# Feed-forward activations turned by VectorE's 32 x 32 blocks and a round trip through DRAM instead of on TensorE

## The chip, the cores and the metric

The kernel runs on one core of a Trainium2 chip. The metric is the device time of one execution in microseconds (us). Within a core TensorE (PE) multiplies, VectorE (DVE) and ScalarE (ACT) work elementwise, GpSimd (POOL) does a few side jobs, and SyncE (SP) issues nearly all DMA transfers, one after the other in program order. PEld is TensorE's weight load, which overlaps its matmuls.

## What is computed

A decoder trunk of two layers on 256 tokens of width 1024 (fp32). Each layer is a feed-forward block, a token mixing block and a second feed-forward block, so there are four feed-forward blocks in all:

```
def swiglu(h, w_gate, w_up, w_down):
    return (jax.nn.silu(h @ w_gate) * (h @ w_up)) @ w_down
for l in range(DEPTH):                                   # DEPTH = 2, FFN_HIDDEN = 2816
    h = rms_norm(x, ffn1_norm[l])
    x = x + 0.5 * swiglu(h, ffn1_w_gate[l], ffn1_w_up[l], ffn1_w_down[l])
    ...                                                  # mixing: S5, sparse and forgetting attention
    h = rms_norm(x, ffn2_norm[l])
    x = x + 0.5 * swiglu(h, ffn2_w_gate[l], ffn2_w_up[l], ffn2_w_down[l])
return rms_norm(x, final_norm)
```

## The kernel before

Every large product is made at more than half precision from two parts: a weight tile `raw` arrives by DMA, ACT copies it to `hi` (rounded), and DVE forms `lo = raw - hi`. The activations are split likewise. TensorE then runs three matmuls (hi x hi, lo x hi, hi x lo) for every 128 rows of the inner dimension and every 128 tokens.

**Units.** `plan` (line 78) cuts all weights into units of at most 2 x 128 rows by 512 columns, in the order of use. `feed_dma` (line 347), `feed_hi` and `feed_lo` issue a unit's load on SP, its `hi` on ACT and its `lo` on DVE. There are 4 `raw` buffers, 5 `hi` and 4 `lo`: a load waits until the `lo` of the unit four earlier is done, a `hi` until TensorE has finished the unit five earlier, a `lo` until it has finished the unit four earlier. A full unit is 512 KB and 12 matmuls of 512 columns.

**Feed-forward block** (`ffn`, line 616). The hidden width 2816 is cut into five chunks of 512 columns and one of 256. For each chunk TensorE makes gate and up products for both halves of the tokens (8 units, 96 matmuls). ACT writes `s` = silu(gate), and DVE writes `act` = up x s (`scalar_tensor_tensor`, two instructions, one for each half of the tokens). The down product needs `act` with the hidden index on the partitions. The generator `up_T` (line 627) brings this about: for every two blocks of 128 hidden columns, four TensorE transposes against the identity `ident` write a PSUM bank `ps_t`, ACT copies the bank to `ath` and DVE writes `atl = ps_t - ath`. `ath` and `atl` are the stationary side of the down product, which runs over d = 0, 1 (two halves of the output columns) and within each over 22 blocks of 128 hidden rows, 11 units.

**Order.** All engines' instructions are written out by hand in program order. Between matmuls `tick` (line 325) asks a model clock (`Clock`) which waiting generator can go on, and steps it. A generator that yields a tile goes on once the model says that the tile is ready. Each engine then runs its own instructions strictly in that order and waits on semaphores for the real data. An ACT or DVE instruction whose data is late holds up the `hi` or `lo` behind it, and a DMA whose data is late holds up the loads behind it on SP. In layer 0's first block, generators that prepare the mixing (`prep_once`, `prep_bias`, `prep_layer`) fill DVE's free time as well.

Of the kernel before, what the change touches and what calls it, by code (L numbers as in the profile page):

```python
# [9 lines left out]
F32 = mybir.dt.float32  # L10
F32R = mybir.dt.float32r
I32 = mybir.dt.int32
AF = mybir.ActivationFunctionType
OP = mybir.AluOpType
# [4 lines left out]
P = 128  # L19
T = 256  # L20
# [3 lines left out]
FK = F // P  # L24
L = 2
H = 6
HD = 64
# [46 lines left out]
def f_chunks():  # L74
    return [(c, min(512, F - c)) for c in range(0, F, 512)]


def plan(a):

    units = []  # L80

    def add(w, k0, nk, c0, n):
        k = k0
        while k < k0 + nk:
            m = min(2 if len(units) > 1 else 1, k0 + nk - k)
            units.append((w[k * P:(k + m) * P, c0:c0 + n].rearrange("(k p) c -> p k c", p=P), m, n))
            k += m

    def ffn(l, which):
        wg, wu, wd = (a[f"{which}_w_{n}"][l] for n in ("gate", "up", "down"))  # L90
        for i, (c0, n) in enumerate(f_chunks()):
            order = [(wg, 0), (wu, 0), (wg, 4), (wu, 4)] if i == 0 else [(wg, 0), (wg, 4), (wu, 0), (wu, 4)]
            for w, k0 in order:
                add(w, k0, 4, c0, n)
        for d in range(2):
            for k0 in range(0, FK, 4):
                add(wd, k0, min(4, FK - k0), d * 512, 512)

    def mix(l):
        w = a["w_in"][l]  # L100
        for k0 in (0, 4):
            add(w, k0, 4, X0, XW)
            add(w, k0, 4, U0, 256)
        for c0, n in ((V0, VW), (QC0, 512), (QC0 + 512, 256), (QB0, 384)):
            for k0 in (0, 4):
                add(w, k0, 4, c0, n)
        for kind, name, d in ORDER:
            if kind == "gate":
                for k0 in (0, 4):
                    add(w, k0, 4, G0 + GATE[name] * D + d * 512, 512)  # L110
            elif kind == "glu":
                add(a["ssm_w_glu"][l], 0, 2, 0, 512)
            else:
                add(a[f"w_branch_{name}"][l], 0, BRANCH_K[name], d * 512, 512)
        for k0 in (0, 4):
            for d in range(2):
                add(a["w_out"][l], k0, 4, d * 512, 512)

    for l in range(L):
        ffn(l, "ffn1")  # L120
        mix(l)
        ffn(l, "ffn2")
    return units
# [110 lines left out]
class Trunk:  # L234
# [381 lines left out]
    def ffn(self, nxt):  # L616
        nc, tc = self.nc, self.tc
        self.hT = self.nexthT
        ss = self.ss
        self.new_ss()  # L620
        with tc.tile_pool(name="ffn", bufs=1, side="left") as pool:
            ath = pool.tile([P, FK, T], F32R, name="ath")
            atl = pool.tile([P, FK, T], F32R, name="atl")
            rstd = None
            pend = None

            def up_T(act, k0, nk):
                yield act
                for b in range(0, nk, 2):
                    i, ps = yield from self.bank()  # L630
                    for j in range(2):
                        for t in range(2):
                            nc.tensor.transpose(ps[:, j * T + t * P:j * T + t * P + P],
                                                act[:, t, (b + j) * P:(b + j + 1) * P], self.ident)
                    yield ps
                    h, lw = ath[:, k0 + b:k0 + b + 2], atl[:, k0 + b:k0 + b + 2]
                    p3 = ps.rearrange("p (k t) -> p k t", k=2)
                    nc.scalar.activation(h, p3, AF.Copy)
                    nc.vector.tensor_tensor(lw, p3, h.bitcast(F32), op=OP.subtract)
                    self.tfree(i)  # L640

            for ci, (c0, n) in enumerate(f_chunks()):
                if ci == 0:
                    self.finish(*self.h_gens[:1])
                    pg = self.acc()
                    self.mm_tok(pg, self.hx, 0, 4, n, 0, 7)
                    pu = self.acc()
                    self.mm_tok(pu, self.hx, 0, 4, n, 0, 7)
                    self.finish(*self.h_gens)
                    self.mm_tok(pg, self.hx, 4, 2, n, 0, 7)  # L650
                    while not self.summed:
                        self.step(self.s_gens[0])
                    rstd = self.rstd_of(ss)
                    self.mm_tok(pg, self.hx, 6, 2, n, 0, 7)
                else:
                    pg = self.acc()
                    self.mm_tok(pg, self.hx, 0, 4, n, 0, 7)
                    self.mm_tok(pg, self.hx, 4, 4, n, 0, 7)
                s = pool.tile([P, 2, 512], F32, tag="s", name="s")
                act = pool.tile([P, 2, 512], F32, tag="act", name="act", bufs=2)  # L660
                for t in range(2):
                    nc.scalar.activation(s[:, t, :n], pg[t][:, :n], AF.Silu, scale=rstd[:, t:t + 1])
                if ci == 0:
                    self.mm_tok(pu, self.hx, 4, 4, n, 0, 7)
                else:
                    pu = self.acc()
                    self.mm_tok(pu, self.hx, 0, 4, n, 0, 7)
                    self.mm_tok(pu, self.hx, 4, 4, n, 0, 7)
                for t in range(2):
                    nc.vector.scalar_tensor_tensor(act[:, t, :n], pu[t][:, :n], rstd[:, t:t + 1], s[:, t, :n],  # L670
                                                   op0=OP.mult, op1=OP.mult)
                if pend:
                    self.finish(pend)
                pend = self.spawn(up_T(act, c0 // P, n // P), -1)
            ax = lambda k: (ath[:, k], atl[:, k])
            gens = []
            for d in range(2):
                ps = self.acc()
                last = nxt is None and d == 1
                for k0 in range(0, FK - LAST if last else FK, 2):  # L680
                    if d == 0 and k0 + 2 > FK - 2:
                        self.finish(pend)
                    self.mm_tok(ps, ax, k0, 2, 512, 0, FK - 1)
                if last:
                    self.last_chunk(ps, ax)
                    return
                gens.append(self.chunk_done(ps, d, 0.5, nxt))
            self.h_gens = [g for g in gens if g]
# [818 lines left out]
```

## Time and profile before

| | |
|---|---|
| median of 3 runs | 1172.56 us (1171.79 to 1173.34) |
| the profiled execution | 1173.79 us, its span 1172.0 us |
| PE busy | 1157.6 us (99%) |
| PEld busy | 973.8 us (83%) |
| DVE busy | 784.0 us (67%) |
| ACT busy | 608.2 us (52%) |
| POOL busy | 85.7 us (7%) |
| DMA | 208.07 MB, mean 178 GB/s; the main queue's packets take 55.5% of the 16 engines' span |

Busy PE is not PE at its peak, since matmuls are pipelined: a matmul of 512 columns is shown as 0.39 us long, but the next one starts 0.227 us later. What a stretch of matmuls costs is therefore read from start to start. The rows used below come from the page, from the waits (who waited for whom), the chain of work that ended last in order of time, the instructions in order of time, the groups of instructions, and the busy times by stretch. L217 is the helper line through which all engine calls go.

### The profile page before, as it was taken

To read this page: it belongs to the slowest core of one execution; us is meant where nothing else is said; L and a number is where in the kernel's file an instruction comes from. 1 tells how busy PE (TensorE), PEld (TensorE's weight loads), DVE (VectorE), ACT (ScalarE), POOL (GpSimd) and SP (SyncE) were. 2 spreads that over 40 slices of the span, in tenths; PEclk is the share of its full clock that TensorE was granted. 3 is DMA by queue.
4 is the path that set the end of the run, shared out by engine and by line. 5 is a ranking of instruction groups with operands and counts; after the bars stand their busy time and mean duration, and the time that the engine had idled before them with its cause. 6 is when DMAs were issued, how large, how long until landed. Compare 5 with 4: busy or idle time off the path is not lost.

```text
span 1172.0 us, 16482 instructions
## 1 busy us (share of the span) xinstructions
PE 1157.6 (99%) x5990; PEld 973.8 (83%) x5990; DVE 784.0 (67%) x1380; ACT 608.2 (52%) x905; POOL 85.7 (7%) x135
## 2 busy tenths in 40 slices
PE   8999999999999999999999999999999999999997
PEld 6888888998787888888888888889987788888885
DVE  4876975798777665555578646558977776555554
ACT  5544454644765554444455545446548655444442
POOL 1000700000210700000000000000013000000000
PEclk9999999999999999999999999999999999999999
DMA  7656655466444666646566546544744456655661
GB/s 270 223 173 178 209 162 178 153 189 183 124 149 152 193 198 190 184 146 223 193 189 181 174 143 221 185 150 146 234 128 140 157 189 197 190 179 162 206 193 69
DMA packets 115554, 208.07 MB, mean 178 GB/s; under 512 B 7486, under 2 KB 27376, under 8 KB 115472
## 3 DMA queue, kind: packets, MB, share of 16 engines
q1 hardware_dynamic: 114000, 203.51, 55.5%
q0 software_dynamic: 1184, 3.11, 1.0%
q8 instruction: 47, 0.77, 0.3%
q10 hardware_dynamic: 288, 0.39, 0.1%
q14 instruction: 35, 0.29, 0.1%
HBM read 205.91 MB, written 1.07 MB: 177 GB/s over the span
## 4 chain that ended last, share of the span: by engine, by line
PE 96%; ACT 2%; DVE 1%; DMA 1%; issue 0%; SPq 0%; ACTq 0%; DVEq 0%
PE ps_acc L217 88%; PE ps_t L217 8%; DMA raw<-in_ffn_w_gate_dram 1%; ACT vT L217 1%; ACT hi L217 0%; ACT st L217 0%; DVE lo L217 0%; SPq L217 0%; DVE st L217 0%; ACT ahl L217 0%; DVE rsqt L217 0%; DVE bl L217 0%; DVE rstd L217 0%; ACT bh L217 0%; ACT junk L217 0%
## 5 line engine op out<-in xcount | busy, mean ns | idle before, releaser
L217 DVE TENSOR_TENSOR lo<-raw,hi 128x1024 fp32r<-128x1024 f32 (+3 forms) x415 | 468.5, 1136 | 228.7 <-PE ps_acc L217 190.2
L217 ACT ACTIVATE hi<-raw 128x1024 fp32r<-128x1024 f32 (+3 forms) x415 | 408.3, 989 | 356.2 <-PE ps_acc L217 278.2
L217 PE MATMUL ps_acc<-hi,h0h 128*128 128x512 f32 (+3 forms) x544 | 212.1, 390 | 2.7 <-ACT hi L217 2.6
L217 PE MATMUL ps_acc<-hi,h1h 128*128 128x512 f32 (+3 forms) x544 | 208.4, 383 | 0.0
L217 PE MATMUL ps_acc<-lo,h0h 128*128 128x512 f32 (+3 forms) x544 | 205.6, 378 | 1.0 <-DVE lo L217 1.0
L217 PE MATMUL ps_acc<-hi,h0l 128*128 128x512 f32 (+3 forms) x544 | 205.2, 377 | 0.0
L217 PE MATMUL ps_acc<-hi,h1l 128*128 128x512 f32 (+3 forms) x544 | 204.3, 376 | 0.0
L217 PE MATMUL ps_acc<-lo,h1h 128*128 128x512 f32 (+3 forms) x544 | 204.2, 375 | 0.0
L217 PE MATMUL ps_acc<-hi,ath 128*128 128x512 f32 x352 | 139.0, 395 | 0.0
L217 PE MATMUL ps_acc<-hi,atl 128*128 128x512 f32 x352 | 137.3, 390 | 0.0
L217 PE MATMUL ps_acc<-lo,ath 128*128 128x512 f32 x352 | 137.2, 390 | 0.0
L217 PEld LDWEIGHTS ps_acc<-hi,h0h 128*128 128x128 f32 x544 | 103.0, 189 | 20.9 <-ACT hi L217 3.9
L217 PEld LDWEIGHTS ps_acc<-lo,h0h 128*128 128x128 f32 x544 | 103.2, 190 | 18.4 <-DVE lo L217 2.3
L217 PEld LDWEIGHTS ps_acc<-hi,h1h 128*128 128x128 f32 x544 | 102.6, 189 | 19.1 <-issue 1.8
L217 PEld LDWEIGHTS ps_acc<-hi,h0l 128*128 128x128 f32 x544 | 103.0, 189 | 18.1
L217 PEld LDWEIGHTS ps_acc<-hi,h1l 128*128 128x128 f32 x544 | 102.5, 188 | 18.0
L217 PEld LDWEIGHTS ps_acc<-lo,h1h 128*128 128x128 f32 x544 | 102.6, 189 | 16.8 <-issue 0.2
L217 PEld LDWEIGHTS ps_acc<-hi,atl 128*128 128x128 f32 x352 | 66.1, 188 | 13.8
L217 PEld LDWEIGHTS ps_acc<-hi,ath 128*128 128x128 f32 x352 | 66.2, 188 | 13.5 <-issue 0.4
L217 PEld LDWEIGHTS ps_acc<-lo,ath 128*128 128x128 f32 x352 | 66.2, 188 | 13.3 <-issue 0.2
L217 DVE TENSOR_TENSOR atl<-ps_t,ath 128x512 fp32r<-128x512 f32 x44 | 30.4, 691 | 28.9 <-ACT ath L217 28.7
L217 ACT ACTIVATE ath<-ps_t 128x512 fp32r<-128x512 f32 x44 | 26.1, 594 | 32.4 <-PE ps_t L217 32.4
(270 smaller groups left out, 1227.8 us busy)
## 6 DMA issues: line engine op xcount, KB each, us to landing
raw<-in_ffn_w_down_dram SPq DMA_DIRECT2D x88, 512.0 KB, 4.3
raw<-in_ffn_w_up_dram SPq DMA_DIRECT2D x80, 512.0 KB, 4.1
raw<-in_ffn_w_gate_dram SPq DMA_DIRECT2D x79, 512.0 KB, 4.3
raw<-in_w_in_dram SPq DMA_DIRECT2D x56, 512.0 KB, 4.6
raw<-in_w_out_dram SPq DMA_DIRECT2D x16, 512.0 KB, 3.7
raw<-in_ffn_w_gate_dram SPq DMA_DIRECT2D x18, 256.0 KB, 2.8
raw<-in_ffn_w_up_dram SPq DMA_DIRECT2D x16, 256.0 KB, 2.8
raw<-in_w_in_dram SPq DMA_DIRECT2D x16, 256.0 KB, 2.8
```

The costliest lines, as they stand in the source:

```text
L217: return f(*args, **kw)
```

## The change

Only `plan` and `ffn` change. The four transposes for each pair of blocks, 176 in all, are gone. `up_T` now runs once for each chunk:

- DVE's `scalar_tensor_tensor` reads gate and up as before but writes `act` with its columns permuted: element (i, m) of 32 x n/32 goes to place m * 32 + i, so that consecutive writes are 32 elements (128 bytes) apart.
- Two DVE `transpose` instructions (one for each half of the tokens) turn the 32 x 32 blocks of `act` within their place into a new tile `at`.
- SP writes `at` to a DRAM tile `actd` in runs of n columns (2 KB; 1 KB in the last chunk), 256 runs.
- SP reads `actd` back into a new tile `aT` (one buffer) in 1024 runs of n/4 columns (512 bytes; 256 bytes in the last chunk), which puts the hidden index on the partitions.
- ACT makes `ath` and DVE `atl` from `aT` (in SBUF) instead of from `ps_t` (in PSUM), as many instructions of the same size as before.

The hidden index that a partition holds is now p * 4 + k within a chunk, so the rows of `w_down` are loaded in that order; the runs of these loads stay 2 KB. `act` has one buffer instead of two. All `up_T` generators of a block are kept in a list, and the down product with d = 0 finishes the one that it needs at every fourth block.

```
-                add(wd, k0, min(4, FK - k0), d * 512, 512)
+                add(wd, k0, min(4, FK - k0), d * 512, 512, "(p k) c -> p k c")
...
             def up_T(act, k0, nk):
+                n, m = nk * P, nk * 32
                 yield act
+                at = pool.tile([P, 2, 512], F32, tag="at", name="at")
+                for t in range(2):
+                    nc.vector.transpose(at[:, t, :n], act[:, t, :n])
+                    yield
+                yield at
+                scr = self.dram.tile([2, P, 512], F32, name="actd")
+                nc.sync.dma_start(bass.AP(tensor=scr.tensor, offset=scr.offset, ap=[[n, P], [P * n, 2], [1, n]]), at[:, :, :n])
+                yield scr
+                aT = pool.tile([P, 8, P], F32, tag="aT", name="aT")
+                nc.sync.dma_start(aT[:, :, :m], bass.AP(tensor=scr.tensor, offset=scr.offset, ap=[[m, P], [32 * n, 8], [1, m]]))
+                yield aT
                 for b in range(0, nk, 2):
-                    i, ps = yield from self.bank()
-                    for j in range(2):
-                        for t in range(2):
-                            nc.tensor.transpose(ps[:, j * T + t * P:j * T + t * P + P],
-                                                act[:, t, (b + j) * P:(b + j + 1) * P], self.ident)
-                    yield ps
-                    h, lw = ath[:, k0 + b:k0 + b + 2], atl[:, k0 + b:k0 + b + 2]
-                    p3 = ps.rearrange("p (k t) -> p k t", k=2)
-                    nc.scalar.activation(h, p3, AF.Copy)
-                    nc.vector.tensor_tensor(lw, p3, h.bitcast(F32), op=OP.subtract)
-                    self.tfree(i)
+                    h, lw = (x[:, k0 + b:k0 + b + 2].rearrange("p k (a j) -> p k a j", a=8) for x in (ath, atl))
+                    a4 = aT[:, :, b * 32:b * 32 + HD].rearrange("p a (k j) -> p k a j", k=2)
+                    nc.scalar.activation(h, a4, AF.Copy)
+                    nc.vector.tensor_tensor(lw, a4, h.bitcast(F32), op=OP.subtract)
+                    yield
...
-                act = pool.tile([P, 2, 512], F32, tag="act", name="act", bufs=2)
+                act = pool.tile([P, 2, 512], F32, tag="act", name="act")
...
-                    nc.vector.scalar_tensor_tensor(act[:, t, :n], pu[t][:, :n], rstd[:, t:t + 1], s[:, t, :n],
-                                                   op0=OP.mult, op1=OP.mult)
-                if pend:
-                    self.finish(pend)
-                pend = self.spawn(up_T(act, c0 // P, n // P), -1)
+                    o, p, g = (x.rearrange(f"p {r} -> p i m", i=32) for x, r in
+                               ((act[:, t, :n], "(m i)"), (pu[t][:, :n], "(i m)"), (s[:, t, :n], "(i m)")))
+                    nc.vector.scalar_tensor_tensor(o, p, rstd[:, t:t + 1], g, op0=OP.mult, op1=OP.mult)
+                ups.append(self.spawn(up_T(act, c0 // P, n // P), -1))
...
-                    if d == 0 and k0 + 2 > FK - 2:
-                        self.finish(pend)
+                    if d == 0 and k0 % 4 == 0:
+                        self.finish(ups[k0 // 4])
```

The order of the instructions changes around each chunk. On PE, in layer 0's second feed-forward block where chunk 1's gate product runs and chunk 0 is transposed (`h0h` and `h0l` are the two parts of the block's input), before:

```order
L217 MATMUL ps_acc<-hi,h0l 128x512
L217 MATMUL ps_t<-ident,act 128x128 x4
L217 MATMUL ps_acc<-hi,h0h 128x512
L217 MATMUL ps_acc<-lo,h0h 128x512
L217 MATMUL ps_acc<-hi,h0l 128x512
L217 MATMUL ps_t<-ident,act 128x128 x4
L217 MATMUL ps_acc<-hi,h0h 128x512
```

After the change no row between the `ps_acc` matmuls of a chunk is left there; the `ps_t` matmuls of that name are gone from the program and nothing takes their place on PE.

On DVE at the same place, from the last `lo` ahead of chunk 0's `act` to chunk 1's `act`, before:

```order
L217 TENSOR_TENSOR lo<-raw,hi 128x1024 x3
L217 SCALAR_TENSOR_TENSOR act<-ps_acc,rstd,s 128x512 x2
L217 TENSOR_TENSOR lo<-raw,hi 128x1024
L217 TENSOR_TENSOR atl<-ps_t,ath 128x512 x2
L217 TENSOR_TENSOR lo<-raw,hi 128x1024 x7
L217 SCALAR_TENSOR_TENSOR act<-ps_acc,rstd,s 128x512 x2
```

and after:

```order
L219 TENSOR_TENSOR lo<-raw,hi 128x1024 x3
L219 SCALAR_TENSOR_TENSOR act<-ps_acc,rstd,s 128x32x16 x2
L219 TENSOR_TENSOR lo<-raw,hi 128x1024
L219 STREAM_TRANSPOSE at<-act 128x512 x2
L219 TENSOR_TENSOR lo<-raw,hi 128x1024 x5
L219 TENSOR_TENSOR atl<-aT,ath 128x512 x2
L219 TENSOR_TENSOR lo<-raw,hi 128x1024 x2
L219 SCALAR_TENSOR_TENSOR act<-ps_acc,rstd,s 128x32x16 x2
```

The block transposes stand where `atl` stood, and `atl` has moved five `lo` back.

On SP, the loads of the same block from its start to chunk 1's up weights, before:

```order
L217 DMA raw<-in_ffn_w_gate_dram 128x2x512 x2
L217 DMA raw<-in_ffn_w_up_dram 128x2x512 x2
L217 DMA raw<-in_ffn_w_gate_dram 128x2x512 x2
L217 DMA raw<-in_ffn_w_up_dram 128x2x512 x2
L217 DMA raw<-in_ffn_w_gate_dram 128x2x512 x4
L217 DMA raw<-in_ffn_w_up_dram 128x2x512 x4
```

and after, from chunk 1's up weights (loaded ahead) to chunk 2's:

```order
L219 DMA raw<-in_ffn_w_up_dram 128x2x512 x4
L219 DMA raw<-in_ffn_w_gate_dram 128x2x512
L219 DMA actd<-at 128x2x512
L219 DMA raw<-in_ffn_w_gate_dram 128x2x512 x2
L219 DMA aT<-actd 128x8x128
L219 DMA raw<-in_ffn_w_gate_dram 128x2x512
L219 DMA raw<-in_ffn_w_up_dram 128x2x512 x4
```

The write and the read of a chunk stand among the loads, with two loads between them. In the mixing blocks the order of ACT and PE is the same as before; in layer 0's first block the preparation's steps move some ten units later.

## Rows read from the trace of the kernel before

**Rows 1.** The page: busy us by engine, granted clock by slice, chain's shares by engine.

```profile
PE 1157.6 (99%) x5990; PEld 973.8 (83%) x5990; DVE 784.0 (67%) x1380; ACT 608.2 (52%) x905; POOL 85.7 (7%) x135
...
PEclk9999999999999999999999999999999999999999
...
PE 96%; ACT 2%; DVE 1%; DMA 1%; issue 0%; SPq 0%; ACTq 0%; DVEq 0%
```

**Rows 2.** Waits, who waited for whom: us in total, times, longest us.

```profile
ACT hi L217 <- PE ps_acc L217: 278.2, 188, 2.6
DVE lo L217 <- PE ps_acc L217: 190.2, 134, 2.4
...
PE ps_acc L217 <- ACT hi L217: 2.6, 1, 2.6
```

**Rows 3.** Chain in order of time, chunk to chunk: start us, us, what.

```profile
450.20 0.44 PE ps_t L217 x4
450.64 0.69 PE ps_acc L217 x3
451.33 0.44 PE ps_t L217 x4
451.76 21.12 PE ps_acc L217 x93
472.88 0.44 PE ps_t L217 x4
```

**Rows 4.** Groups by form, PE and ACT: xcount | busy us, mean ns | idle before.

```profile
L217 PE MATMUL ps_t<-ident,act 128*128 128x128 f32 x176 | 26.6, 273 | 0.0
L217 ACT ACTIVATE ath<-ps_t 128x512 fp32r<-128x512 f32 x44 | 26.1, 594 | 32.4 <-PE ps_t L217 32.4
L217 ACT ACTIVATE hi<-raw 128x512 fp32r<-128x512 f32 x58 | 36.5, 630 | 60.5 <-PE ps_acc L217 45.6 <-issue 10.6 <-DMA raw<-in_w_in_dram 1.6
```

**Rows 5.** Groups by form on DVE, same columns.

```profile
L217 DVE TENSOR_TENSOR lo<-raw,hi 128x512 fp32r<-128x512 f32 x58 | 39.9, 689 | 32.0 <-PE ps_acc L217 26.2 <-issue 2.9 <-ACT hi L217 1.7
L217 DVE SCALAR_TENSOR_TENSOR act<-ps_acc,rstd,s 128x512 f32<-128x512 f32 x40 | 28.5, 749 | 14.9 <-PE ps_acc L217 14.9
L217 DVE COPY vT<-v 32x128 f32<-32x128 f32 x16 | 5.0, 314 | 0.2
L217 DVE SCALAR_TENSOR_TENSOR ahl<-av,ahl 128x512 fp32r<-128x512 f32 x2 | 2.2, 1118 | 1.4 <-ACT ahl L217 1.4
L217 DVE TENSOR_SCALAR q<-q 128x512 f32<-128x512 f32 x2 | 0.9, 427 | 0.5 <-ACT q L217 0.5
L217 DVE COPY kt<-ps_t 32x128 f32<-32x128 f32 x2 | 0.6, 291 | 0.4 <-ACT kt L217 0.4
```

**Rows 6.** DVE in order of time, chunk 1: start us, us, what.

```profile
447.52 1.43 DVE L217 SCALAR_TENSOR_TENSOR act<-ps_acc,rstd,s 128x512 f32<-128x512 f32 x2 [0.98 <-PE ps_acc L217]
...
457.10 1.23 DVE L217 TENSOR_TENSOR lo<-raw,hi 128x1024 fp32r<-128x1024 f32 x1 [1.50 <-PE ps_acc L217]
459.82 1.23 DVE L217 TENSOR_TENSOR lo<-raw,hi 128x1024 fp32r<-128x1024 f32 x1 [1.49 <-PE ps_acc L217]
```

**Rows 7.** Weight loads of 428 to 590 us, by tile `raw`.

```profile
DMA to landing us min/median/max: 2.7/3.8/5.4
```

**Rows 8.** DMA issues of 447 to 515 us: xcount, KB each, median us to landing.

```profile
raw<-in_ffn_w_up_dram SPq DMA_DIRECT2D x9, 512.0 KB, 3.6
...
raw<-in_ffn_w_up_dram SPq DMA_DIRECT2D x3, 256.0 KB, 2.8
```

**Rows 9.** Busy us (x) by stretch: PE, PEld, DVE, ACT, POOL, PEclk, DMA share, GB/s.

```profile
30.00:160.00 130.00, 130.00 (x642) 108.13 (x641) 102.23 (x212) 65.01 (x81) 22.48 (x42) 1.00 0.63 195
428.00:506.00 78.00, 78.00 (x359) 64.71 (x358) 43.07 (x42) 38.12 (x44) 0.00 (x0) 1.00 0.60 179
510.00:524.00 14.00, 14.00 (x96) 12.95 (x95) 7.47 (x11) 6.38 (x11) 0.00 (x0) 1.00 0.49 139
```

More of the change, by code (lines that the diff above doesn't have):

```diff
@@ L80, in plan, with add @@
     units = []
-    def add(w, k0, nk, c0, n):
+    def add(w, k0, nk, c0, n, rows="(k p) c -> p k c"):
         k = k0
+        part = w[k0 * P:(k0 + nk) * P, c0:c0 + n].rearrange(rows, p=P)
         while k < k0 + nk:
             m = min(2 if len(units) > 1 else 1, k0 + nk - k)
-            units.append((w[k * P:(k + m) * P, c0:c0 + n].rearrange("(k p) c -> p k c", p=P), m, n))
+            units.append((part[:, k - k0:k - k0 + m], m, n))
             k += m
@@ L624, in ffn @@
             rstd = None
-            pend = None
+            ups = []
             def up_T(act, k0, nk):
+                n, m = nk * P, nk * 32
                 yield act
-                for b in range(0, nk, 2):
-                    i, ps = yield from self.bank()
-                    for j in range(2):
-                        for t in range(2):
-                            nc.tensor.transpose(ps[:, j * T + t * P:j * T + t * P + P],
-                                                act[:, t, (b + j) * P:(b + j + 1) * P], self.ident)
-                    yield ps
-                    h, lw = ath[:, k0 + b:k0 + b + 2], atl[:, k0 + b:k0 + b + 2]
-                    p3 = ps.rearrange("p (k t) -> p k t", k=2)
-                    nc.scalar.activation(h, p3, AF.Copy)
-                    nc.vector.tensor_tensor(lw, p3, h.bitcast(F32), op=OP.subtract)
-                    self.tfree(i)
+                at = pool.tile([P, 2, 512], F32, tag="at", name="at")
[9 more added lines that the diff above has]
+                yield aT
+                for b in range(0, nk, 2):
+                    h, lw = (x[:, k0 + b:k0 + b + 2].rearrange("p k (a j) -> p k a j", a=8) for x in (ath, atl))
[3 more added lines that the diff above has]
+                    yield
             for ci, (c0, n) in enumerate(f_chunks()):
```

## The prediction

> **What bounds the kernel now.** I read the chain that ended last first. TensorE holds 96% of it, and the page gives PE 1157.6 us of the 1172.0 us span, at a granted clock shown as 9 (90% or more) in every slice [rows 1]. Busy PE alone proves little, so I looked next at the waits for who is late. ACT's `hi` waited for TensorE 278.2 us in 188 places and DVE's `lo` 190.2 us in 134 places, each to get a buffer back. The other way round, the largest wait of PE is 2.6 us, once [rows 2]. So the split engines and the loads run ahead of TensorE and are held back by it. In the chain in order of time a chunk of the feed-forward block is nothing but PE: from 450.20 to 472.88 us, 22.68 us, of which 21.12 + 0.69 = 21.81 us are the 96 matmuls (0.227 us each) and two times 0.44 us the transposes [rows 3]. Nothing else stands in the period. What leaves PE leaves the time, as long as nobody else becomes late.
>
> **What goes from PE.** 176 transposes go, in 44 groups of four [rows 4]. Their mean of 273 ns is not the price, since they overlap. The price is the 0.44 us that a group holds in the chain: 44 x 0.44 = 19.4 us. The four groups of the 256-column chunks cost the same, as they are the same four instructions. I allow 0.43 to 0.45 us for a group, 18.9 to 19.8 us. They stood on the path, with a wait of zero ahead of them, so the whole sum counts. A gain beyond it has no source: the remaining matmuls are the same in number and shape, and PE hardly waits for anything.
>
> **What DVE gets.** For each full chunk two block transposes of 128 x 512. No row shows one. The cheapest row of that size is a one-input SBUF operation, 427 ns; the dearest is 1118 ns; the nearest in price that reads and writes fp32 in SBUF at one element after another is `lo` 128 x 512, 689 ns [rows 5], and I take that. The two `act` instructions (749 ns) now write 128 bytes apart. The nearest row is `vT`, which writes 16 bytes apart: 314 ns for 128 elements, against 291 ns for `kt`, which writes them densely [rows 5]; 23 ns more for 128 elements is 0.09 us for 512. The upper end I set at twice the time, 0.75 us more. A gain is excluded here, since instructions are only added and lengthened. A chunk therefore adds 2 x 0.69 + 2 x 0.09 = 1.6 us to DVE, between 0.9 and 2 x 1.12 + 2 x 0.75 = 3.7 us. What hides it: in 428 to 506 us DVE is busy 43.1 of 78 us [rows 9], so 10 us of each 22.68 us are free. There it costs nothing even at the upper end. The exception is layer 0's first block, where the mixing's preparation fills DVE: 102.2 of 130 us in 30 to 160 us [rows 9]. Six chunks add 9 us there, which makes 112 of some 125 us, still free by a tenth; at the upper end 22 us, which makes 125 of 125. That end is a rival below.
>
> [...]
>
> **ATH and ATL.** Their count and size stay. They now read SBUF instead of PSUM. ACT's `hi` of that size takes 630 ns from SBUF where `ath` took 594 [rows 4], 44 x 36 ns = 1.6 us on an engine that is half idle: nothing on the path.
>
> **The round trip.** It adds waits on SP, ACT and DVE, each with something queued behind it. In the changed order the write is issued when the block transposes are done, two loads follow, then the read, which waits on SP for the write to land, with all later loads behind it. The load just ahead of the read refills the buffer that the third `lo` after the block transposes frees; `lo` come 2.72 us apart (457.10 to 459.82) [rows 6], so the read cannot go out before some two periods after the write, 5.4 us. The write has 256 runs of 2 KB like a weight load, and those land in 3.8 us, 5.4 at most [rows 7]. SP loses nothing then, at worst a fraction of a us, and the loads behind it have `raw` and `hi` buffers of several units ahead of them.
>
> The read has as many bytes in 1024 runs. If bytes count, it lands like a load in 3.8 us. A row between: a load of 256 runs of 1 KB lands in 2.8 us [rows 8]. At the shares of [rows 9], 2 KB take 2048 / (179 / 0.60 / 16 GB/s) = 110 ns of a DMA engine and 1 KB 1024 / (139 / 0.49 / 16) = 58 ns. So bytes set the price down to 1 KB. With 64 runs for each of 16 engines the read takes 1.8 us of them by bytes, 3.7 us if 512 bytes cost what 1 KB does, and 7.0 us if they cost what 2 KB do. It lands after 3.8, 2.8 + 3.7 - 0.9 = 5.6, or 3.8 + 7.0 - 1.8 = 9.0 us. I take 5.6, from the nearest row. What covers it: `atl` stands five `lo` after the block transposes, two after the read, so 5.4 us pass before DVE comes to it, and a little less before ACT comes to `ath`. A later read holds up the `hi` and `lo` behind it, but TensorE then has four `lo` buffers, 4 x 2.72 = 10.9 us, less the `lo` just done (1.2), one `ath` (0.6), two `atl` (1.4) and the next `lo` (1.2): 6.4 us. PE waits only if the read lands later than 5.4 + 6.4 = 11.8 us. All three values lie below.
>
> At the end of the up products the last chunk's chain has more: the down product with d = 0 reaches its blocks after 20 others, 20 x 6 x 0.227 = 27 us, and the chain is some 3 us of DVE, a write and a read. Of `act` with one buffer, the next chunk's write comes 22 us after the block transposes that read it, on the same engine. The `w_down` rows in another order keep 2 KB runs, which I cost at nothing. What is late next once the 19.4 us are gone: nobody; PE stays at 99%.
>
> **Rivals.**
>
> 1. *Layer 0's first block pays.* DVE is full there at the upper ends, and a `lo` behind a long instruction reaches PE. Of the 27.8 us in which DVE is idle there now, a quarter stays as waits that nothing covers, some 7 us: 1172.6 - 19.4 + 7 = 1160 us. Against it, 112 of 125 us at the rows I take.
> 2. *The DMA engines become the bound (slower).* In a chunk they need 4.19 MB at 298 GB/s, 14.1 us, and 1.8 us for the write. The read adds 64 runs of p ns. Up to p = 92 ns this stays under the new period of 21.8 us; from p = 106 ns it exceeds the old one, 22.68 us, and the kernel is slower. At p = 125 ns a full chunk takes 23.9 us, 1.2 us more than before; 20 of them give 1172.6 + 24 = 1197 us. For it: only that short runs can have a fixed price, which no row shows below 1 KB. Against it: 1 KB costs 58 ns, so 512 bytes would have to cost twice that.
> 3. *The read lands late by its pattern (slower).* Beyond 11.8 us each us costs 24 chunks one us, so from 11.8 + 19.4 / 24 = 12.6 us the kernel is slower; at 20 us, it takes 1172.6 - 19.4 + 24 x 8.2 = 1350 us. Against it, no load in this stretch lands after more than 5.4 us [rows 7], and my upper end is 9.0. [...]
> 4. *The gap is not PE's.* The slots of the transposes could be filled by a wait for `lo` or `hi` that they hide now: 1172 us, no change. Against it, [rows 2]: the splits wait for PE.
>
> **How the numbers follow.** The profiled execution took 1173.8 us with a span of 1172.0. Its span becomes 1172.0 - 19.4 = 1152.6, its time 1154.4; it lies 1.2 us above the median, so the median becomes 1172.56 - 19.4 = 1153.2 us. Its own range is 1151.5 (0.45 us for a group, and the spread of a us between runs) to 1156 (0.43 and some 2 us of short waits). Chances: forecast 0.67, rival 1 0.20 (1156 to 1165), rival 2 0.08 (0.02 of it between 92 and 106 ns, still faster), rival 3 0.02, rival 4 0.03. The range from 1151 to 1163 leaves out the slow cases and the far end of rival 1. A measurement of this kernel can tell about 0.2% from no change, 2.3 us. Faster by more: 0.67 + 0.20 + 0.02 = 0.89; within: 0.03; slower: 0.08.
>
> **What would show it.** Right: a chunk's period in the chain of 21.8 us with no `ps_t` piece, `hi` and `lo` still waiting for `ps_acc`, no wait of PE for `lo` in any feed-forward block, block transposes near 0.7 us, reads landing in 4 to 7 us and a DMA share near 0.75 to 0.85 in the chunks. Wrong: waits of PE for `lo` between 30 and 160 us (rival 1); SP waiting long at the read, reads landing after more than 11.8 us, or a DMA share at 0.95 (rivals 2 and 3); a period of 22.6 us with PE idle where the transposes were (rival 4).

## The result: 1159.3 us, and where the gain stopped

| | before | after |
|---|---|---|
| median of 4 runs each | 1172.95 us (1171.79 to 1174.02) | 1159.3 us (1156.85 to 1163.26) |
| ratio | | 0.9883, 95% interval 0.987 to 0.9897 |
| the profiled execution, its span | 1173.79, 1172.0 us | 1161.18, 1159.4 us |
| DMA | 208.07 MB, 178 GB/s | 231.11 MB, 199 GB/s |

The kernel became 13.7 us faster. 19.4 us were forecast, to 1153.2 us. The profile is that of one execution, 1161.18 us; by the two spans it is 12.6 us faster than before, a little less than the medians say. The page of after, to be read beside [rows 1] (busy us by engine, granted clock by slice, the chain's shares):

```profile
PE 1139.0 (98%) x5814; PEld 956.0 (82%) x5814; DVE 815.2 (70%) x1426; ACT 606.0 (52%) x907; POOL 84.4 (7%) x135
...
PEclk9999999999999999999999999999999999999999
...
PE 82%; DMA 7%; DVE 6%; ACT 3%; issue 2%; SPq 0%; DVEq 0%; ACTq 0%
```

TensorE held 96% of the chain before and holds 82% now. So somewhere in the program another engine ends last. The waits of after, beside [rows 2] (us in total, times, longest us):

```profile
ACT hi L219 <- PE ps_acc L219: 203.7, 146, 3.3
...
DVE lo L219 <- PE ps_acc L219: 94.3, 66, 2.4
DVE atl L219 <- ACT ath L219: 59.8, 21, 4.8
...
ACT ath L219 <- DMA aT<-actd: 46.8, 24, 4.4
```

Before, DVE's wait at `atl` was shorter and in smaller pieces, and ACT's `ath` waited for the transposes [rows 4]:

```profile
DVE atl L217 <- ACT ath L217: 28.7, 37, 1.9
```

The splits still wait mostly for TensorE, but `lo` only half as long as before, and ACT, with DVE behind it, now waits for the read of `aT`. TensorE's own waits in 30 to 210 us, which is all of layer 0's first block but its start:

```profile
PE ps_t L219 <- DVE x L219: 3.7, 1, 3.7
PE ps_t L219 <- DMA toe<-reld: 2.1, 1, 2.1
```

Before, neither wait is there. `x` is the block's output; the transposes that wait for it make the mixing's input. `toe` is a table of the mixing's bias, read back from DRAM by POOL's queue.

**Block by block.** DVE's last `x<-ps_acc` ends a block. The first block's is this row, of before:

```profile
204.82 1.37 DVE L217 SCALAR_TENSOR_TENSOR x<-ps_acc,x 128x512 f32<-128x512 f32 x2 [1.52 <-PE ps_acc L217]
```

and of after:

```profile
207.64 1.37 DVE L219 SCALAR_TENSOR_TENSOR x<-ps_acc,x 128x512 f32<-128x512 f32 x2 [1.52 <-PE ps_acc L219]
```

From such rows, each stretch in us from the end of the one before:

| | before | after | |
|---|---|---|---|
| layer 0, first feed-forward block | 204.8 | 207.6 | +2.8 |
| mixing | 198.6 | 198.7 | +0.1 |
| layer 0, second block | 185.8 | 180.8 | -5.0 |
| layer 1, first block | 190.5 | 185.1 | -5.4 |
| mixing | 198.7 | 198.6 | -0.1 |
| layer 1, second block, to the end of its output | 185.6 | 180.5 | -5.1 |

The sum is -12.6 us, which is the difference of the two spans. Three blocks gain 5.0 to 5.4 us for 11 groups, 0.46 to 0.49 us each, where 0.44 was forecast. With their mean gain the first block would have gone to 204.8 - 5.1 = 199.7 us; it went to 207.6. **The whole shortfall lies in layer 0's first block: 7.9 us against the other blocks.** Against the forecast this execution lacks 19.4 - 12.6 = 6.8 us, less than that, because the other three blocks gained 0.9 us more than forecast.

In the other blocks a chunk looks as forecast. DVE in order of time, one chunk of layer 0's second block:

```profile
449.49 2.18 DVE L219 SCALAR_TENSOR_TENSOR act<-ps_acc,rstd,s 128x512 f32<-128x512 f32 x2 [0.96 <-PE ps_acc L219]
...
452.63 1.30 DVE L219 STREAM_TRANSPOSE at<-act 128x512 f32<-128x512 f32 x2
...
466.34 1.29 DVE L219 TENSOR_TENSOR atl<-aT,ath 128x512 fp32r<-128x512 f32 x2 [1.52 <-ACT ath L219]
...
471.25 2.17 DVE L219 SCALAR_TENSOR_TENSOR act<-ps_acc,rstd,s 128x512 f32<-128x512 f32 x2 [0.99 <-PE ps_acc L219]
```

From `act` to `act` 21.76 us instead of 22.68 [rows 3]. DVE waits 1.52 us at `atl` for the read, and `act` still waits for TensorE afterwards: that wait costs nothing here.

The new and changed instructions (groups by form: xcount | busy us, mean ns of one | idle before):

```profile
L219 DVE SCALAR_TENSOR_TENSOR act<-ps_acc,rstd,s 128x512 f32<-128x512 f32 x40 | 43.2, 1166 | 10.4 <-PE ps_acc L219 10.4
...
L219 DVE STREAM_TRANSPOSE at<-act 128x512 f32<-128x512 f32 x40 | 25.8, 686 | 0.0
L219 ACT ACTIVATE ath<-aT 128x512 fp32r<-128x512 f32 x44 | 25.6, 625 | 46.8 <-DMA aT<-actd 46.8
```

`act` takes 1166 ns instead of 749 [rows 5], a block transpose 686 ns, `ath` 625 instead of 594 [rows 4]. The reads of `aT` land after

```profile
DMA to landing us min/median/max: 3.2/5.2/9.2
```

and the writes of `actd` after 3.9/5.6/7.9 us. By stretch, beside [rows 9]:

```profile
30.00:160.00 130.00, 127.90 (x601) 105.64 (x600) 102.45 (x207) 60.96 (x77) 21.18 (x42) 1.00 0.73 233
428.00:506.00 78.00, 78.00 (x346) 64.59 (x345) 51.04 (x51) 38.58 (x43) 0.00 (x0) 1.00 0.76 234
```

In the chunks DVE went from 43.1 to 51.0 us and the DMA share from 0.60 to 0.76. In 30 to 160 us DVE is as busy as before (102.45 against 102.23 us), although it got more to do there: what it did not get done moved behind 160 us.

**What ends last in the first block.** DVE's wait at `atl` in 30 to 165 us, before and after:

```profile
DVE atl L217 <- ACT ath L217: 7.0, 6, 1.9
```

```profile
DVE atl L219 <- ACT ath L219: 20.2, 6, 4.8
```

The chain of after, in order of time, the start of each piece, its us, and what it is:

```profile
139.33 7.70 DMA raw<-in_ffn_w_down_dram
147.13 1.07 ACT hi L219
148.21 0.08 SPq L219
148.39 4.22 DMA aT<-actd
152.64 0.64 ACT ath L219
...
154.06 0.68 DVE biasT L219
...
168.24 1.22 DVE lo L219
169.45 0.61 DVE pm L219
170.15 0.55 issue
170.70 1.21 DVE lo L219
171.94 0.69 DVE bp L219
172.66 1.30 DVE x L219 x2
```

From `ath` on the chain runs over DVE alone until `x`: `lo` and the preparation's `pm`, `cx` and `bp`, one behind the other (11.73 of the 12 us in 160 to 172 us are busy). TensorE at that place:

```profile
169.27 0.39 PE L219 MATMUL ps_acc<-hi,atl 128*128 128x512 f32 x1
173.40 1.50 PE L219 MATMUL ps_t<-ident,x 128*128 128x128 f32 x4 [3.74 <-DVE x L219]
174.56 0.78 PE L219 MATMUL ps_acc<-hi,ath 128*128 128x512 f32 x1
175.13 0.63 PE L219 MATMUL ps_acc<-lo,ath 128*128 128x512 f32 x1
175.56 0.63 PE L219 MATMUL ps_acc<-hi,atl 128*128 128x512 f32 x1
```

It waits 3.74 us for `x`, and then its matmuls start 0.43 to 0.57 us apart instead of 0.227. The granted clock fell at the same place (the column behind POOL's; then DMA share and GB/s):

```profile
169.00:173.40 4.40, 0.66 (x3) 0.20 (x2) 4.30 (x7) 0.43 (x2) 0.00 (x0) 0.84 0.75 202
173.40:179.00 5.60, 5.47 (x17) 4.35 (x18) 3.56 (x7) 4.44 (x10) 0.00 (x0) 0.51 0.54 169
179.00:190.00 11.00, 11.00 (x58) 9.15 (x57) 4.94 (x5) 5.55 (x7) 0.00 (x0) 1.00 0.52 160
```

It is 0.51 over the 5.6 us behind the wait (0.50 in each us from 173.40 to 178.40), and 1.00 in the 11 us after them, where the matmuls from 179.16 to 183.72 us start 0.22 to 0.24 us apart. So the 7.9 us come apart into 3.7 us of waiting for `x`, 2.1 us of waiting for `toe`, and a remainder of 2.1 us. The clock of 0.51 behind the wait for `x` is enough for it: the two groups of transposes and nine matmuls from 173.40 to 179.16 us take 5.76 us, where 2 x 0.44 + 9 x 0.227 = 2.9 us is their price at a granted clock of 1.00 [rows 3], [rows 9], 2.8 us less (an estimate from these rows).

### The profile page after: what moved, and what is told of

The parts are those of the page before. It is cut to its first block, busy times and chain, and to the rows that moved or that the text cites. A ratio compares the mean times of both kernels' runs of the same rounds, so it can differ in the third digit from the quotient of the medians.

```text
span 1159.4 us, 16226 instructions
## 1 busy us (share of the span) xinstructions
PE 1139.0 (98%) x5814; PEld 956.0 (82%) x5814; DVE 815.2 (70%) x1426; ACT 606.0 (52%) x907; POOL 84.4 (7%) x135
## 2 busy tenths in 40 slices
DMA packets 147040, 231.11 MB, mean 199 GB/s; under 512 B 12350, under 2 KB 53744, under 8 KB 146960
## 4 chain that ended last, share of the span: by engine, by line
PE 82%; DMA 7%; DVE 6%; ACT 3%; issue 2%; SPq 0%; DVEq 0%; ACTq 0%
PE ps_acc L219 76%; PE ps_t L219 6%; DVE lo L219 2%; DMA aT<-actd 2%; DMA actd<-at 2%; DMA raw<-in_ffn_w_down_dram 1%; DVE act L219 1%; ACT hi L219 1%; DMA xT<-in_l_xT_dram 1%; DMA x<-in_x_dram 1%; ACT vT L219 1%; DVE at L219 0%; SPq L219 0%; DVE atl L219 0%; ACT st L219 0%
## 5 line engine op out<-in xcount | busy, mean ns | idle before, releaser
L219 PE MATMUL ps_acc<-hi,h0h 128*128 128x512 f32 (+3 forms) x544 | 207.4, 381 | 1.8 <-ACT hi L219 1.8
L219 PE MATMUL ps_acc<-hi,h1h 128*128 128x512 f32 (+3 forms) x544 | 207.6, 382 | 0.0
L219 PEld LDWEIGHTS ps_acc<-hi,h1h 128*128 128x128 f32 x544 | 102.5, 188 | 18.9 <-issue 1.5
L219 DVE TENSOR_TENSOR atl<-aT,ath 128x512 fp32r<-128x512 f32 x44 | 29.0, 697 | 59.8 <-ACT ath L219 59.8
L219 DVE SCALAR_TENSOR_TENSOR act<-ps_acc,rstd,s 128x512 f32<-128x512 f32 (+1 forms) x48 | 48.0, 1085 | 10.4 <-PE ps_acc L219 10.4
```

The costliest lines, as they stand in the source:

```text
L219: return f(*args, **kw)
```

## The experiments

The shortfall could come from reads that land late and hold DVE up at `atl` (theory B where an expectation uses a letter), or from DVE's own added work together with the preparation (theory C). The planning clock that writes the order can be wrong about either.

**Only the first block, only the others.** `TRIP` names the blocks that use the round trip; the others keep the transposes on TensorE.

```
+TRIP = (0,)            # e1_first_only;  (1, 2, 3) in e2_later_only
...
+        trip = self.blk in TRIP
...
+                ups.append(self.spawn((up_T if trip else pe_T)(act, c0 // P, n // P), -1))
```

> The round trip in layer 0's first feed-forward block alone; the other three blocks transpose on TensorE as in the kernel before. Theory (the round trip pays in three blocks and costs in this one, since DVE is full of preparation there): slower than the kernel before by some 4 us, about 1177 us, with a wait of PE for x near 170 us and a stretch at the lower granted clock behind it. Rival A (the shortfall is spread over all four blocks): this block gains a quarter of what the changed kernel gains, 13.7 / 4 = 3.4 us, about 1169.5 us.

Measured: 1175.57 us (1172.77 to 1178.9, 11 runs) against 1172.91, ratio 1.0022 (1.0012 to 1.0031).

> The reverse: layer 0's first block transposes on TensorE as before, the other three go through DRAM. Theory: three blocks gain 3 x 5.1 = 15.4 us, about 1157.5 us, with the spread between runs as small as the kernel before has it (some 2 us) since the place that varies is gone. Rival A: three quarters of 13.7 us, about 1162.7 us.

Measured: 1159.41 us (1157.1 to 1160.13, 4 runs), ratio 0.9881 (0.9867 to 0.9894), between the two expectations. In its profiled execution the first block ends at 204.5 us as before and the later blocks gain as in after, but the second mixing takes 200.2 instead of 198.7 us; there the granted clock was 0.60 in 888 to 892 us, where before has 1.00.

So the change pays in the later blocks and costs in the first one. The place is shown; the cause is not yet.

**The read planned later.** The planning clock lets a DMA land 1.8 us after its bytes, which makes 3.3 us for these transfers; measured are 5.2 and 5.6 us. With 4.0 instead of 1.8 for `actd` and `aT` the plan comes to 5.5 us.

```
-            done = start + cost + (1.8 if eng == "dma" else 0)
+            done = start + cost + ((4.0 if x.tensor.name.startswith(("actd", "aT")) else 1.8) if eng == "dma" else 0)
```

> The changed kernel, but the model clock that sets the order is told that the write and the read take 4.0 us to land instead of 1.8; so ath and atl stand one or two units later in ACT's and DVE's order, and the read one load later on SP. No instruction is added or removed. Theory B (in layer 0's first block ACT and DVE stand at ath and atl because the read lands later than the order assumes, and the time lost there makes x late): the waits of ACT for aT, 46.8 us in all, go mostly away, the wait of PE for x (3.7 us) goes too, about 1153 us. Theory C (DVE has too much work there, wherever it waits): x stays late, 1158 to 1160 us.

Measured: **1152.71 us** (1151.91 to 1153.53, 4 runs), ratio 0.9827 (0.9814 to 0.9841), the fastest version here. TensorE has no wait for `x` or `toe`, DVE waits at `atl` 4.4 us in 30 to 165 us instead of 20.2, and the block ends at

```profile
200.04 1.37 DVE L219 SCALAR_TENSOR_TENSOR x<-ps_acc,x 128x512 f32<-128x512 f32 x2 [1.52 <-PE ps_acc L219]
```

That is the whole gain, and the time is what the prediction had forecast (1153.2 us). It speaks for late reads, but the order of everything else in the block moved too.

**`act` written densely.** The strided write is left out (the permutation with it, so the values land in other places).

```
...
-                    nc.vector.scalar_tensor_tensor(o, p, rstd[:, t:t + 1], g, op0=OP.mult, op1=OP.mult)
+                    nc.vector.scalar_tensor_tensor(act[:, t, :n], pu[t][:, :n], rstd[:, t:t + 1], s[:, t, :n], ...)
```

> The changed kernel with act written densely instead of 128 bytes apart; it leaves the column permutation out, so that the values behind it are others. The order of the instructions is the same. DVE has 48 x 0.33 = 16 us less to do, some 4 us of it in layer 0's first block. Theory C (DVE's work): x comes some 4 us earlier and PE's wait for it goes, about 1153 us. Theory B (late reads): the waits for aT stay, so DVE waits longer at atl instead; 1157 to 1159 us.

Measured: 1156.69 us (1155.27 to 1159.09, 4 runs), 0.9868 (0.9853 to 0.9883). `act` is back at 747 ns, the first block ends at 201.7 us, and TensorE's waits in it fell from 5.8 to 2.9 us (`toe` 1.7, `x` 1.2); 12.3 us of waiting at `atl` are left. That lies between the two theories: DVE's work is a part of the cause, and not the whole.

**A read that needn't wait for the write.** It takes its bytes from `w_out` (so other values arrive) while the planning clock counts it as before.

```
-                nc.sync.dma_start(aT[:, :, :m], bass.AP(tensor=scr.tensor, offset=scr.offset, ap=[[m, P], [32 * n, 8], [1, m]]))
...
+                self.clock.put("dma", P * 8 * m * 4 / 360e3, [aT[:, :, :m]], [back])
+                other = self.a["w_out"][0]
+                nc.sync.eng.dma_start(aT[:, :, :m], bass.AP(tensor=other.tensor, offset=other.offset, ap=[[m, P], [32 * n, 8], [1, m]]))
```

> The changed kernel in exactly its order on every engine, but the read takes the same runs from a weight tensor instead of actd, so that it doesn't wait on SP for the write to land; the activations behind it are therefore others. The write is still made. Theory B (ACT and DVE stand at ath and atl because the read lands late): the read goes out up to 2 to 4 us earlier, ACT's 19 us and DVE's 20 us of such waits between 30 and 165 us fall by half or more, PE's wait for x goes, 1153 to 1155 us. Theory C (DVE's work and the preparation's steps bunched just ahead of x, which this kernel leaves as they are): PE still waits 2 to 4 us for x, 1157 to 1160 us.

Measured: 1160.89 us (1158.12 to 1165.98, 6 runs), 0.99 (0.9882 to 0.9918). The run tells nothing about late reads, since the reads hardly came earlier. In the first block they went out sooner behind the write in four chunks of six, by 0.4 to 2.7 us (46.24 - 42.35 = 3.9 instead of 48.28 - 41.72 = 6.6 us in the first); in the last two they went out after some 8 to 9 us as before. They landed after 6.6 us (median) instead of 5.2, and 18.9 us of waiting at `atl` stayed. It shows something else. TensorE waited 3.1 us for `toe` this time, and behind that wait the clock fell as it fell behind `x` in after:

```profile
144.00:152.00 8.00, 7.11 (x17) 4.79 (x17) 5.96 (x7) 3.28 (x4) 7.69 (x14) 0.57 0.83 277
```

**The preparation moved forward; the strided `act` priced; the read planned later still.**

```
-TICK, BACKLOG, PREP, EAGER = 1.5, 8.0, 0.0, -0.2
+TICK, BACKLOG, PREP, EAGER = 1.5, 8.0, 2.0, -0.2                                   # e6_prep_earlier
...
+        if op == "scalar_tensor_tensor" and "act" in out.tensor.name and len(out.shape) == 3:
+            return 0.155 + n * 1.8e-3                                              # e7_priced_act
...
+            done = start + cost + ((6.0 if x.tensor.name.startswith(("actd", "aT")) else 1.8) if eng == "dma" else 0)   # e8
```

> The changed kernel with the preparation of the mixing allowed to run 2 us ahead of TensorE in the model's order (before: 0): its last steps on DVE stand some nine units earlier, at lo 61 instead of 70, and ath and atl of layer 0's first block one unit later. Theory C (preparation bunched ahead of x): PE's wait for x goes, 1153 to 1155 us. Theory B: the waits at atl shrink only by the one unit; where DVE is fuller before 150 us, lo is late there, 1155 to 1160 us.

Measured: 1158.37 us (1157.7 to 1160.67, 4 runs), 0.9879 (0.9867 to 0.9892). Only 2.7 us of waiting at `atl`, but TensorE now waits 2.3 us for POOL's `dbl` from 155.8 us on, and the clock is 0.79 in 156 to 164 us.

> The changed kernel, but the model clock prices the strided act at 1.08 us for 512 columns, as measured, instead of 0.75; nothing else is told to it. ath and atl move by one or two units in three of layer 0's six chunks, the preparation hardly moves. Theory B: the shortfall shrinks with the waits at atl, in part, 1155 to 1158 us. Theory C: DVE has the same work, 1158 to 1160 us.

Measured: 1154.31 us (1154.03 to 1155.29, 4 runs), 0.9843 (0.983 to 0.9855). 10.2 us of waiting at `atl` are left, but TensorE waits only 1.1 us, for `x`. Better than both theories had it.

> As the kernel whose model was told 4.0 us for the landings, with 6.0 us: ath and atl stand one or two units later again, past the measured landing of 5.2 us. Theory B: the waits of ACT for aT fall from 20 us to nearly none, but they reached PE nowhere already, so the time stays, 1152 to 1154 us. If the order of the preparation decided instead (its last step stands at lo 73 here, later than in the changed kernel), PE waits for x again, 1156 to 1160 us.

Measured: 1159.83 us (1158.35 to 1163.06, 5 runs), 0.9896 (0.9882 to 0.991). Waits at `atl` of 1.5 us, and yet TensorE waits 2.9 us for `x` and 1.2 us for `toe`; clock 0.79 in 172 to 180 us.

Theory B falls with e8 (hardly any waits at `atl`, no gain) and with e7 (10 us of them, nearly the whole gain); theory C falls as the only cause with e3. What separates the good runs from the bad ones is neither wait of DVE but whether TensorE, whose order is fixed (in after, e4 and e5 its matmuls of 30 to 205 us stand in the same order, with 5.8, 2.9 and 3.1 us of waits), meets a product that is not ready. That was the theory of the last four runs.

> The changed kernel with both corrections of the planning clock: the round trip's landing counted at 1.8 + 2.2 us more (e3_read_late) and the strided act counted at 1.08 instead of 0.75 us (e7_priced_act). Theory 'the plan of layer 0's first block runs ahead of the chip, and TensorE's fixed order then meets products that are late': with both, that block takes 200 us as in e3, which is the whole gain, so nothing is left to win: 1152 to 1153.5 us, and DVE's idle time at atl in 30 to 165 us stays under 5 us. Rival 'e3 and e7 hit two good orders by chance': any order can come out, 1154 to 1160 us.

The edit is that of e3 and that of e7 together. Measured: 1155.89 us (1153.32 to 1158.6, 5 runs), 0.9853 (0.9838 to 0.9869). The profiled execution, 1153.32 us, did as expected: 3.2 us of waiting at `atl`, the block's end at 199.7 us. The median is above the expectation and lies in the rival's range, that e3 and e7 hit good orders by chance; the run does not rule this out. The other executions have no trace, only their mean granted clock: 0.998 in the one of 1153.32 us and 0.993 in that of 1158.6 us.

> The changed kernel in its own order; the eight pm and bp products of layer 0's second half of the preparation (8 x 0.69 = 5.5 us of DVE in 160 to 172 us) are left out, while the planning clock still counts them. Part of the mixing's operator is therefore zero. Theory 'DVE's work just ahead of the end of layer 0's first block decides': x comes 4 us earlier, TensorE's 3.7 us wait for it and the low granted clock behind it are gone, 1154 to 1156 us. Rival 'reads that land late decide': the DVE idle time at atl (20 us) stays, DVE still comes late to what TensorE waits for, 1158 to 1160 us.

```
+            tt = charge if l == 0 and dst is bp else nc.vector.tensor_tensor
```

(`charge` counts the instruction in the planning clock and issues nothing.) Measured: 1158.29 us (1154.24 to 1158.63, 4 runs), 0.9864 (0.9847 to 0.988). By its median it looks like the rival; by its trace it is not. The wait for `x` is gone and the first block ends at 201.9 us, with one wait of TensorE left in it:

```profile
PE ps_t L219 <- DMA toe<-reld: 2.2, 1, 2.2
```

The 1158.63 us of that execution hold 1.7 us that are lost elsewhere, in the first mixing (200.4 instead of 198.7 us), where the clock was at 0.57 for one stretch, behind waits of at most 0.5 us:

```profile
316.00:320.00 4.00, 3.26 (x24) 2.33 (x21) 3.31 (x12) 3.45 (x11) 0.00 (x0) 1.00 0.46 139
320.00:324.00 4.00, 4.00 (x22) 3.88 (x20) 2.02 (x8) 2.55 (x9) 2.75 (x3) 0.57 0.74 236
```

Another 1.6 us are lost in layer 1's first block, where TensorE waits 0.7 us for a `lo`; the rest of that loss is not explained.

> The changed kernel in its own order; the read of actd takes 128 runs of 4 KB instead of 1024 runs of 512 bytes (the values land in other places, so the permutation is left out). If short runs have a price, as the prediction's 5.6 us for the read against 3.8 us for a load has it, the median landing of aT falls from 5.2 to about 4 us, the DMA share in 428 to 506 us from 0.76 to about 0.68, and the waits at atl in layer 0's first block from 20 us to under 12: 1155 to 1158 us. Rival 'the landing is set by bytes and by what else is in the queues': it stays at 5 us or more, the share at 0.74 or more, and the time at 1158 to 1160 us.

```
-                nc.sync.dma_start(aT[:, :, :m], bass.AP(tensor=scr.tensor, offset=scr.offset, ap=[[m, P], [32 * n, 8], [1, m]]))
+                nc.sync.dma_start(aT[:, :, :m], bass.AP(tensor=scr.tensor, offset=scr.offset, ap=[[8 * m, P], [m, 8], [1, m]]))
```

Measured: 1158.6 us (1156.26 to 1159.71, 4 runs), 0.9872 (0.9858 to 0.9885). The landing of `aT`:

```profile
DMA to landing us min/median/max: 3.4/4.6/6.9
```

4.6 us for 4 KB runs against 5.2 for 512 bytes, with a DMA share of 0.73 in 30 to 162 us in both. Short runs have a price here, but a small one, 0.6 us, between the two expectations; 15.0 us of waiting at `atl` and 2.6 us for `toe` stay.

**The two waits of TensorE taken away, the late reads left.** As e10, with the products of `toe` 15 matmuls later.

```
-        yield from self.units_on(6)
+        yield from self.units_on(8)
```

> As e10_no_bp (the eight pm and bp products left out), and the three products with toe in the preparation of the bias stand 15 matmuls later on TensorE (3.4 us), so that TensorE asks for toe after it has landed. Both waits that TensorE had in layer 0's first block, for x and for toe, have then lost their cause; the reads land as late as before. Theory 'only the two waits of TensorE and the granted clock behind them cost time; DVE's idle time at atl by itself costs nothing': no wait of TensorE over 0.8 us in that block, x at its end at 199.5 to 200.5 us (e10: 201.9), 1153.5 to 1156 us, though DVE still idles 15 to 20 us at atl. Rival 'late reads cost time by themselves, by way of lo': a new wait of TensorE for lo or hi of over 1 us, the block's end at 201.5 us or later, 1156.5 to 1159 us.

Measured: 1154.78 us (1152.26 to 1155.57, 5 runs), 0.9845 (0.9832 to 0.9859). Of TensorE's waits in 30 to 210 us one is left,

```profile
PE ps_acc L219 <- DVE lo L219: 0.4, 1, 0.4
```

while DVE still waits at `atl` nearly as long as in after,

```profile
  ACT ath L219: 18.4, 6
```

and the block ends earlier than in any other kernel:

```profile
199.54 1.37 DVE L219 SCALAR_TENSOR_TENSOR x<-ps_acc,x 128x512 f32<-128x512 f32 x2 [1.52 <-PE ps_acc L219]
```

The rival, that late reads cost time by themselves, is out: 18.4 us of waiting for them cost nothing once DVE has 5.5 us less to do behind them and TensorE is not made to wait.

**All profiled executions with the round trip in the first block, side by side.** The end of the first block against TensorE's waits in 30 to 210 us and the granted clock of the 5.6 to 8 us behind such a wait, where it fell:

| | waits of TensorE, us | DVE waits at `atl`, us | granted clock behind a wait | end of the block, us |
|---|---|---|---|---|
| after | 5.8 (`x`, `toe`) | 20.2 | 0.51 | 207.6 |
| e1 | 4.4 (`x`, `toe`) | 16.8 | 0.79 | 206.6 |
| e5 | 3.1 (`toe`) | 18.9 | 0.57 | 206.0 |
| e8 | 4.1 (`x`, `toe`) | 1.5 | 0.79 | 205.8 |
| e6 | 2.9 (`dbl`, `toe`, `bp`) | 2.7 | 0.79 | 203.8 |
| e11 | 3.4 (`toe`, `x`) | 15.0 | 1.00 | 202.7 |
| e10 | 2.2 (`toe`) | 19.6 | 1.00 | 201.9 |
| e4 | 2.9 (`toe`, `x`) | 12.3 | 1.00 | 201.7 |
| e7 | 1.1 (`x`) | 10.2 | 1.00 | 200.4 |
| e3 | 0 | 4.4 | 1.00 | 200.0 |
| e9 | 1.4 (`x`) | 3.2 | 1.00 | 199.7 |
| e12 | 0.4 (`lo`) | 18.4 | 1.00 | 199.5 |

DVE's waits do not order the last column. TensorE's waits come much nearer, though not one by one (e5 waits less than e11 and ends later): with the clock beside them, what the last column has above 199.7 us is at most 0.3 us more than TensorE's waits where the clock stayed up, and 1.2 to 3.2 us more where it fell. Where it stayed up the waits can also cost less than their length: 1.4 us in e9 show in nothing.

## Why the prediction was right and where it failed

**Right: the price on TensorE.** 0.44 us for a group, 0.46 to 0.49 measured in three blocks; a chunk's period of 21.8 us, 21.76 measured; nobody takes the gain back there. And the whole 19.4 us can be had: e3, with the same instructions in another order, took 1152.71 us.

**Right: the block transposes and the read.** 0.69 us taken from `lo`, 0.686 measured. 5.6 us for the read, 5.2 measured (median), 9.2 at most against an upper end of 9.0. The DMA share in the chunks is 0.76, within 0.75 to 0.85. No `lo` reaches TensorE late by more than 0.8 us, as the 11.8 us of cover had it (its terms add up to 11.9: 10.9 less 4.4 is 6.5, not 6.4, which changes nothing). That the read's number fits is in part luck: the sum gave short runs 1.8 us over a load, and e11 shows 0.6. The rest is that loads landed later too, with the DMA share up from 0.60 to 0.76; the weight loads of 428 to 590 us, beside [rows 7]:

```profile
DMA to landing us min/median/max: 2.8/4.4/8.8
```

**Mis-sized: the strided `act`.** +0.09 us was taken from `vT`, which writes 16 bytes apart and 128 elements; measured is 1166 - 749 = 0.42 us, a rise of 56%. The rows taken do not even give the sign: `vT`'s mean of 314 ns holds a copy of 715 ns, the median of its 16 is 274, below `kt`'s 291, and `kt` reads PSUM where `vT` reads SBUF. That the forecast had a rise at all was luck. `vT` in the trace of before (ns, min/median/max):

```profile
L217 DVE COPY vT<-v x16: 261/274/715, 312.2 to 889.1; 32x128 f32<-32x128 f32 x16
```

The bound, +0.75, held. In e4 the same instruction takes 747 ns when it writes densely.

**Wrong: that SP loses nothing.** The write was to land before the read's turn. It lands after 5.6 us in the median, 7.9 at most, and SP waited 26.9 us in 17 places for it before it could issue the read. In the later blocks that cost nothing that the time shows.

**The step that failed: DVE's budget in layer 0's first block.** The text came to "112 of some 125 us, still free by a tenth". It counted the added instructions and not the waits in front of them. In the trace of after DVE starts nothing past a waiting `atl`: a step of the preparation whose inputs `e` it had itself finished by 48.84 us starts at 57.41 us, behind an `atl` that waited 4.76 us. So an `atl` that waits for its read takes DVE's time from everything behind it. Needed were 10 x 0.42 = 4.2 us more for `act`, 7.3 us in all for `at` (6.5 and 0.8), and 20.2 us of waiting at `atl` (7.0 of them there before, among the idle time), 31.7 us, against the 27.8 us in which DVE was idle. The 3.9 us too many are near the 3.7 us for which TensorE waited for `x`: the last steps of the preparation came when `x` was due. With 5.5 us of them left out (e10) that wait is gone. The budget is not the only way to a late `x`: in e8 DVE waits 1.5 us at `atl` and TensorE still 2.9 us for `x`, in another order. The time, 1159.3 us, lies outside the forecast's own range (1151.5 to 1156 us) and in that of rival 1, which named the place and its price (7 us left, 1160 us) with a chance of 0.20. That its number fits is luck: a quarter of the idle time was a guess, and the way was another, not a `lo` behind a long instruction, but `x` behind the preparation, with `toe` and the clock beside it.

**Not seen: what TensorE's order asks for outside the chain.** "What is late next: nobody" looked at `hi` and `lo` only. `toe` is a read of 768 KB that landed 5.9 us after its issue before the change and 7.8 us after it, with a DMA share of 0.94 in 140 to 148 us. Its issue had also moved from 124.4 to 134.9 us, and TensorE came to it 5.8 us after the issue instead of 10.0: 2.1 us too early. And no term allowed for what followed a wait of TensorE: a remainder of about 2 us, with the granted clock at 0.51 over 5.6 us.

**Why the plan did not absorb it.** The order is made by a model clock that took 3.3 us for the landings and 0.75 us for `act`. Corrected for either (e3, e7) it wrote an order in which TensorE hardly waits; corrected too far for the landings (e8) it wrote one as slow as after. That a true plan always does is not shown: the median with both corrections is 3.2 us above e3's (0.9853 against 0.9827), and where its longer executions lost their time is open, as they left no trace (the longest, 1158.6 us, had a mean granted clock of 0.993).

**The rivals that stayed out.** The DMA engines did not become the bound in the chunks (a share of 0.76), and no read of after landed later than 9.2 us. The 512-byte runs have a price of 0.6 us on a landing (5.2 us against 4.6 in e11). And the slots of the transposes hid no other wait.

## What to carry to other kernels

On an engine that works in order, a wait is work: in a stretch where an engine has no slack, count the idle time that a new dependence puts in front of an instruction as if it were the instruction's own (here 20.2 us at `atl`, where 27.8 us had been idle). Then ask which instructions of the bounding engine need something from that engine that comes only once, since the delay surfaced there (3.7 us for `x`), not at the steady stream (at most 0.8 us for a `lo`). And where an order is written by a model clock, give it the measured price of each new operation before the change is judged: here the landings' alone were worth another 6.6 us (e3, 1152.71 us), `act`'s alone 5.0 (e7, 1154.31), and both together 3.4 (e9, 1155.89). That they do not add up says that the price helps but does not make the order.

## What the runs showed of the hardware

- A wait of TensorE of 3.7 us (after) or 3.1 us (e5) is followed by 5.6 or 8 us at a granted clock of 0.51 or 0.57; waits of 2.1 us in after and 2.6 us in e11 (for `toe`) are not (1.00), and one of 2.3 us in e6 (for `dbl`) is, less deeply (0.79 over 8 us). In the mixing the clock fell to 0.57 and 0.60 for 4 us in one profiled execution each of e10 and e2, and stayed at 1.00 in both mixings of before, after, e3 and e6. What decides this is left open.
- The slowest execution of e5, 1165.98 us, had the lowest mean granted clock, 0.989, against 0.995 in the fastest, 1158.12 us; but one of 1162.21 us had 0.997, so the clock is not the whole difference.
- A two-input DVE instruction of 128 x 512 fp32 that writes 128 bytes apart takes 1166 ns (after), and 747 ns when it writes densely (e4).
- A block transpose of 128 x 512 fp32 takes 686 ns (after), as much as `lo`, an elementwise instruction with two inputs (689 ns [rows 5]).
- In e5, where the reads did not wait for the write (and read another tensor), they took longer to land: the median went from 5.2 to 6.6 us, with a DMA share of 0.80 in 132 to 160 us against 0.78 in after.
